# Gate projections token-major, in seven half-size products per branch, in a hybrid decoder block on one core

## The chip, the core and the metric

The kernel runs on one core of one Trainium2 chip. The metric is device microseconds of one execution. TensorE (PE) multiplies matrices, VectorE (DVE) and ScalarE (ACT) work on tiles, GpSimd (POOL) does the same and issues DMAs that add into a tile, SyncE (SP) issues the plain DMA loads. Times are in us unless marked ns.

## The reference

One layer over 512 tokens of 1024 channels. All weights and activations are float32.

```python
h = rms_norm(x, g_mix)
p = h @ w_in                       # 1024 -> 9*512 + 3*1024
q, fp, iv, go, bg, cg, xc, u, v, gates = split(p)
o_a, o_b, o_c = hgrn2(q, fp, iv, go), short_conv(bg, cg, xc), spatial_gate(u, v)
y = einsum('snw,nwd->snd', [o_a, o_b, o_c], w_branch)   # 3 branches, each 512 -> 1024
gate = sigmoid(gates).reshape(S, 3, 1024)
merged = sum(gate * y, axis=branch)
x = x + merged @ w_o
x = x + square(relu(rms_norm(x, g_ffn) @ w_ff1)) @ w_ff2
return rms_norm(x, g_final)
```

The change concerns `gates` (512 x 1024 by 1024 x 3072), `y` (three times 512 x 512 by 512 x 1024) and `merged`.

## The kernel before

**A float32 product in three.** Each operand is split into a high part, rounded to fp32r by a copy on ACT, and a low part, the rest, by a subtraction on DVE. `mm3` issues three matmuls: high by high, high by low, low by high. One matmul has a stationary block of 128x128 and moves 512 columns into a PSUM bank of 128x512.

**Units.** The kernel is a list `units`, worked off in order, each with a matmul part and a read-out for later. A usual unit is one 512 KB weight block: 8 blocks of 128x128, 24 matmuls. In order: units 0 to 3 and 4 to 7 (two projections of the recurrence), 8 to 11 (values), 12 to 15 (u), 16 to 19 (output gate), 20 to 31 (the convolution's three projections), and then, for each of the 8 blocks d of 128 output channels, five units: gate projections of branches 1, 2, 0 (24 matmuls each), `w_bc` (branches 1 and 2, 24) and `w_a` (branch 0, 12). These are units 32 to 71, channel-major: a tile is 128 channels by 512 tokens. `ev_gate` multiplies by the norm's factor `rb` and takes the sigmoid; `ev_bc` and `ev_a` multiply the branch results by the gates and add; `ev_a` leaves the merged tile split in high and low. The output projection (8 units) and the feed-forward part follow, the latter already in half-size products whose weight sums are added by DMA.

**Order of the queues.** It is written by hand (`manual_schedule`), so each engine does what the loop issues, in that order. For unit i the loop issues: the high split (ACT) of the weight block that a unit needs next, the read-out of unit i-1, the low split (DVE), other work hung on `pre`, one weight load (SP), the matmuls of unit i, and work hung on `post`. A weight block goes through a ring of three raw tiles and a ring of three pairs `wh`/`wl`; PSUM has eight banks (`acc`). Tiles named h, x, z and tmp are slots in fixed places that later stages use again, so a new owner waits until the last reader of the old one is done.

Of the kernel before, what the change touches and what calls it, by code (L numbers as in the profile page):

```python
# [7 lines left out]
F32 = mybir.dt.float32  # L8
# [3 lines left out]
ALU = mybir.AluOpType  # L12
# [21 lines left out]


@with_exitstack
def trunk_kernel(ctx: ExitStack, tc, xT, x_t, w_f, w_t, w_bc, w_a, w_o, w_1, w_2, vecs, rows, gfin, w_sg, cst, lmask, out):
# [22 lines left out]
    def zpair(i, dt):  # L60
        return rp.tile([P, 2 * S], dt, tag=f"z{i}", name=nm("z"))
# [59 lines left out]
    def tmp(w=S, dt=F32):  # L121
        return wp.tile([P, S + 64], dt, tag="tmp", name=nm("tmp"), bufs=6)[:, :w]
# [408 lines left out]
    def branch(w, o0, n):  # L531
        a = acc()
        for k in range(4):
            mm3(a, w[0][:, o0 + k * P:o0 + (k + 1) * P], w[1][:, o0 + k * P:o0 + (k + 1) * P],
                zt[n][k][0], zt[n][k][1], k == 0, k == 3)
        return a
# [6 lines left out]
    def ev_a(d, a):  # L543
        tt(dve, part[0], a, part[0], ALU.mult)
        tt(dve, part[0], part[0], part[1], ALU.add)
        mt = hslot(d, F32R)
        act.activation(mt[:, :S], part[0], AF.Copy)
        yield
        tt(dve, mt[:, S:], part[0], f(mt[:, :S]), ALU.subtract)
        mg.append((mt[:, :S], mt[:, S:]))  # L550


    for h in range(NH):
# [13 lines left out]
    for d in range(KD):  # L567
        for n in (1, 2, 0):
            proj(28 + n * KD + d, lambda a, d=d, n=n: ev_gate(d, n, a))
        unit(w_bc[d], lambda w: (branch(w, 0, 1), branch(w, S, 2)), lambda a, d=d: ev_bc(d, a))  # L570
        unit(w_a[d], lambda w: branch(w, 0, 0), lambda a, d=d: ev_a(d, a), S)

    at(pre, 3, sg_rows)
    at(pre, 4, sg_rows2)
# [39 lines left out]
    at(pre, 21, go_sig)  # L614


    x2, x2h, x2l = [], [], []
# [226 lines left out]
    at(pre, o0, reload_x)  # L844
    at(post, o0 + 4, turn, range(4))
    at(pre, o0 + 5, turned, range(4))
    f0 = len(units)
# [16 lines left out]
    at(pre, f0 + 4, ffn_rows)  # L864
    at(pre, f0 + 5, ev_1, 0)
    at(pre, f0 + 5, ev_1, 1)

    W11, W12, W21, W22 = (0, 0), (0, 1), (1, 0), (1, 1)

    def early(u):  # L870

# [91 lines left out]
    raws, ws = {}, {}  # L963
    order = [x for s in sorted(when) for x in when[s]]
    issued = [0]

    def issue():
        if issued[0] < len(order):
# [4 lines left out]
            issued[0] += 1  # L973

    def split_hi(i):
        n = loads[i][1]
# [198 lines left out]
```

## Time and profile before

| | us |
|---|---|
| runs | 829.84, 829.08, 829.73 |
| median of the runs | 829.73 |
| profiled execution, its own time | 829.28 |
| its span in the profile | 827.5 |
| PE busy | 816.4 (99%) |
| DVE busy | 544.0 (66%) |
| ACT busy | 346.0 (42%) |
| POOL busy | 156.7 (19%) |
| mean granted clock, of full speed | 0.997 |
| moved by DMA | 102.45 MB |

The span is that of one profiled execution on the chip; its own time is longer by what lies around the span. Matmuls overlap, so that PE counts as busy from the first to the last of a row without a gap. The order of reading is: which engine is busy, what the chain of work that ended last consists of, what that engine waited for, and then how full the others are in the stretch that is changed, here about 244 to 461 us after the start. Rows of all these views stand further down.

### The profile page before, as it was taken

Reading aid. Unit: us, or ns where it says so; the run is one execution under the profiler, and the core shown is the slowest. Engines: PE = TensorE matmul, PEld = TensorE weight load, DVE = VectorE, ACT = ScalarE, POOL = GpSimd, SP = SyncE. Lnnn points to the kernel's source line nnn. Section 1 sums busy time; section 2 is a strip of 40 time slices with the busy share of each in tenths; the row PEclk is TensorE's granted clock in tenths of the full one; section 3 lists DMA queues with packets and bytes.
Section 4 is the critical chain, followed back from the end, with each engine's and each line's share of the span. In section 5 each row is a group of like instructions: output and inputs, shape, how many; then the busy total and the mean of one; then the engine's idle time right before and its main releaser. Section 6 shows DMA issues by size and latency. Waiting matters only on the chain.

```text
span 827.5 us, 9867 instructions
## 1 busy us (share of the span) xinstructions
PE 816.4 (99%) x3798; PEld 680.7 (82%) x3798; DVE 544.0 (66%) x706; ACT 346.0 (42%) x519; POOL 156.7 (19%) x187
## 2 busy tenths in 40 slices
PE   9999999999999999999999999999999999999995
PEld 7888888888988888888888888888888888888884
DVE  7456999878664445544444445777777777777763
ACT  7467555364333223223232335343434343434332
POOL 4312644663220000000000010202020202020000
PEclk9999999999999999999999999999999999999998
DMA  8422222212122232222325345748384838383502
GB/s 309 127 80 75 76 102 77 77 52 95 60 63 103 91 113 90 90 93 98 115 89 204 103 160 145 216 115 231 99 222 113 248 85 251 83 250 87 162 0 102
DMA packets 30431, 102.45 MB, mean 124 GB/s; under 512 B 3504, under 2 KB 3888, under 8 KB 30384
## 3 DMA queue, kind: packets, MB, share of 16 engines
q1 hardware_dynamic: 20736, 67.45, 23.4%
q0 software_dynamic: 9360, 34.08, 16.7%
q8 instruction: 30, 0.49, 0.2%
q10 hardware_dynamic: 288, 0.29, 0.1%
q14 instruction: 17, 0.14, 0.1%
HBM read 99.71 MB, written 2.10 MB: 123 GB/s over the span
## 4 chain that ended last, share of the span: by engine, by line
PE 93%; DVE 3%; issue 2%; DMA 1%; ACT 0%; SPq 0%; POOLq 0%; POOL 0%; DVEq 0%
PE acc L98 29%; PE acc L99 29%; PE acc L100 29%; PE acc L330 2%; PE acc L1065 1%; DVE h L79 1%; DVE wl L79 1%; DVE h L307 1%; DMA raw<-w_t 1%; PE acc L485 0%; PE acc L386 0%; PE acc L648 0%; PE acc L388 0%; PE acc L369 0%; PE acc L328 0%
## 5 line engine op out<-in xcount | busy, mean ns | idle before, releaser
L98 PE MATMUL acc<-x,wh 128*128 128x512 f32 x672 | 263.9, 393 | 0.3 <-DVE h L339 0.3
L100 PE MATMUL acc<-x,wl 128*128 128x512 f32 x672 | 261.7, 389 | 0.0
L99 PE MATMUL acc<-x,wh 128*128 128x512 f32 x672 | 261.7, 389 | 0.0
L979 ACT ACTIVATE wh<-raw 128x1024 fp32r<-128x1024 f32 (+1 forms) x114 | 116.7, 1025 | 237.4 <-PE acc L99 134.6
L79 DVE TENSOR_TENSOR wl<-raw,wh 128x1024 fp32r<-128x1024 f32 (+1 forms) x120 | 153.6, 1282 | 44.0 <-ACT wh L979 43.9
L98 PEld LDWEIGHTS acc<-x,wh 128*128 128x128 f32 x672 | 126.2, 188 | 26.4 <-DVE h L339 0.5
L100 PEld LDWEIGHTS acc<-x,wl 128*128 128x128 f32 x672 | 126.2, 188 | 26.3
L99 PEld LDWEIGHTS acc<-x,wh 128*128 128x128 f32 x672 | 126.2, 188 | 25.6 <-issue 0.2
L79 DVE TENSOR_TENSOR h<-h,acc 128x512 f32<-128x512 f32 x118 | 75.7, 682 | 11.1 <-PE acc L100 11.0
L79 DVE TENSOR_TENSOR z<-z,z 128x1024 fp32r<-128x1024 f32 x51 | 61.6, 1220 | 32.1 <-ACT z L773 32.1
L79 DVE TENSOR_TENSOR h<-h,h 128x256 f32<-128x256 f32 (+4 forms) x89 | 67.9, 767 | 7.6 <-ACT h L752 3.6
L699 ACT ACTIVATE h<-tmp 128x512 f32<-128x512 f32 x32 | 20.3, 633 | 125.8 <-DVE tmp L698 125.8
L773 ACT ACTIVATE z<-z 128x1024 fp32r<-128x1024 f32 x51 | 53.1, 1052 | 44.8 <-PE acc L100 28.1
L100 PE MATMUL acc<-z,h 128*128 128x512 f32 x184 | 71.6, 389 | 0.0
L98 PE MATMUL acc<-z,h 128*128 128x512 f32 x184 | 71.6, 389 | 0.0
L99 PE MATMUL acc<-z,h 128*128 128x512 f32 x184 | 71.6, 389 | 0.0
L79 DVE TENSOR_TENSOR tmp<-acc,rb 128x512 f32<-128x512 f32 x28 | 19.4, 691 | 78.2 <-PE acc L100 78.2
L769 POOL DMA_DIRECT2D z<-w x28 | 24.5, 875 | 233.1 <-DVE z L79 194.5
L79 POOL TENSOR_TENSOR tmp<-tmp,tmp 128x512 f32<-128x512 f32 x15 | 19.9, 1324 | 198.8 <-DVE tmp L79 185.9
L698 DVE SCALAR_TENSOR_TENSOR tmp<-acc,rb 128x512 f32<-128x512 f32 x32 | 22.0, 688 | 30.8 <-PE acc L100 30.8
L98 PEld LDWEIGHTS acc<-z,h 128*128 128x128 f32 x184 | 34.5, 188 | 7.2
L100 PEld LDWEIGHTS acc<-z,h 128*128 128x128 f32 x184 | 34.5, 188 | 7.2
(190 smaller groups left out, 1066.3 us busy)
## 6 DMA issues: line engine op xcount, KB each, us to landing
z<-w POOLq DMA_DIRECT2D x65, 512.0 KB, 6.2
raw<-w_f SPq DMA_DIRECT2D x52, 512.0 KB, 3.2
raw<-w SPq DMA_DIRECT2D x34, 512.0 KB, 5.5
raw<-w_bc SPq DMA_DIRECT2D x8, 512.0 KB, 3.2
raw<-w_o SPq DMA_DIRECT2D x8, 512.0 KB, 3.3
raw<-w_t SPq DMA_DIRECT2D x4, 512.0 KB, 3.2
raw<-w_a SPq DMA_DIRECT2D x8, 256.0 KB, 2.6
h<-x_t SPq DMA_DIRECT2D x4, 512.0 KB, 6.8
```

The lines of the kernel that those rows point to most:

```text
L79: return e.tensor_tensor(out=o, in0=a, in1=b, op=op)
L98: pe.matmul(o, lh, rh, start=start, stop=False, skip_group_check=more)
L99: pe.matmul(o, lh, rl, start=False, stop=False, skip_group_check=more)
L100: pe.matmul(o, ll, rh, start=False, stop=stop, skip_group_check=more)
L307: dve.reciprocal(e[:, 256:], e[:, :256])
L330: pe.matmul(ps[:, cs(b)], kl[:, cs(b)], qk[:, cs(b)], start=True, stop=True)
L698: dve.scalar_tensor_tensor(out=t, in0=part["f", i], scalar=0.0, in1=part["r2b"], op0=ALU.max, op1=ALU.mult)
L699: act.activation(hf["a" if r < 2 else "b"][:, cs(r % 2, S)], t, AF.Square)
L769: pool.dma_start(wr[n, g], w_2[g, src[0], src[1]], accum_op=ALU.add)
L773: act.activation(hi, wr[src, g], AF.Copy)
L979: act.activation(hi[:, :n], raws[i][:, :n], AF.Copy)
L1065: pe.matmul(a4[t], lh, rh, start=j == 0 and rnd == 0, stop=j == KD - 1 and rnd == 2)
```

## The change

The gates and the branch products become token-major: a tile is 128 tokens by channels, x is the stationary operand and the weight moves. For each branch the gate projection is a 2 x 2 block product, 512 tokens by 1024 in halves, 1024 x 1024 weights in halves, done in seven products of half size (Strassen, in Winograd's form) with sums of the blocks of x and of the weights. With W11 to W22 for a branch's weight quarters, c is W12 to which W11, then W22, then W21 are added, and t3 is W12 plus W22. Each quarter is two raw blocks of 512 KB (g = 0, 1).

- **Order of the units.** Units 32 to 35 are the branch products of branch 1, 36 to 39 those of branch 2, both kept in SBUF. Units 40 to 46 are the seven gate products of branch 1, 47 to 53 of branch 2, 54 to 60 of branch 0, in the order p1, p5, p2, p6, p3, p7, p4 (weights W11, t1, W21, t2, W22, t3, t4, where t1, t2 and t4 are c after one, two and three additions, and p2 and p3 use raw quarters). Units 61 to 65 are branch 0's product, the last block of 24 matmuls cut into two units of 12. The output projection starts at unit 66.
- **x.** `x_load` fetches x again (8 loads), `x_norm` multiplies by weight and norm factor, `x_form` makes seven blocks or sums for each of two halves and splits them, hung on units 30 to 38.
- **Weights.** `g_load` loads raw quarters through the raw ring, `g_chain` starts c or t3 by a plain load, `g_add` adds a quarter by a DMA on POOL's queue, `g_split` splits one unit ahead of its product: three of four pairs in the rings `wh`/`wl`, the fourth in slots h0/h1. p1, p6, p7 and p4 add up in one pair of PSUM banks (B) and are read out in between, p5 and p3 in another (C), p2 has its own (A).
- **Read-out.** `g_ev` copies p1 and p5 to SBUF (`gt`), adds the next products to them and takes the sigmoid. `merge` multiplies a branch's kept product by its gates, `merge_add` adds two branches, `y_ev` of branch 0 multiplies and adds the last. `m_turn` turns the merged tiles by 32 transposes of 128x128 on PE, `m_turned` splits them.
- **Loads of later weights** stop at `phase1` and go on from unit 55 (`issue_more`).

In the diff "..." marks what is left out.

```diff
-    def ev_gate(d, n, a):
-        g = tmp()
-        part[n] = g
-        tt(dve, g, a, rb, ALU.mult)
-        act.activation(g, g, AF.Sigmoid)
...
-    def ev_bc(d, a):
-        for i, n in enumerate((1, 2)):
-            tt(dve, part[n], a[i], part[n], ALU.mult)
-        tt(pool, part[1], part[1], part[2], ALU.add)
...
+    def x_norm(g):
+        for b in range(4):
+            xv = xr_[b // 2][:, cs(b % 2, S)]
+            dve.scalar_tensor_tensor(out=xv, in0=xv, scalar=vcol(V_GMIX + 4 * g + b), in1=rb, op0=ALU.mult, op1=ALU.mult)
...
+    def x_form(g, *names):
...
+                i0, i1, op = {"1": (q(0, 1), q(1, 1), ALU.subtract), "2": (xr_.get("1"), q(0, 0), ALU.subtract),
+                              "4": (xr_.get("2"), q(1, 0), ALU.add), "3": (q(0, 0), q(0, 1), ALU.subtract)}[n]
+                tt(dve, src[n], i0, i1, op)
+        for n in names:
+            t = hslot(XT[g, n], F32R)
+            xf[g, n] = (two(t[:, :S]), two(t[:, S:]))
+            act.activation(xf[g, n][0], src[n], AF.Copy)
+        for n in names:
+            tt(dve, xf[g, n][1], src[n], f(xf[g, n][0]), ALU.subtract)
...
+    def g_chain(n, kind, base):
+        for g in range(2):
+            gw[n, g, kind] = xpair(base + g, F32)
+            nc.sync.dma_start(gw[n, g, kind], w_g[n, g, 0, 1])
+
+    def g_add(n, kind, fi, c):
+        for g in range(2):
+            pool.dma_start(gw[n, g, kind], w_g[n, g, fi, c], accum_op=ALU.add)
+
+    def g_split(n, name, src):
+        for g in range(2):
+            i = gn[0]
+            gn[0] += 1
+            if i % 4 < 3:
+                hi = wp.tile([P, 2 * S], F32R, tag="wh", name=nm("wh"))
+                lo = wp.tile([P, 2 * S], F32R, tag="wl", name=nm("wl"))
+            else:
+                hi, lo = hslot(0, F32R), hslot(1, F32R)
+            r = gw[(n, g) + src]
+            act.activation(hi, r, AF.Copy)
+            tt(dve, lo, r, f(hi), ALU.subtract)
...
+    def g_product(n, a, b, key, start):
...
+        for j in range(2):
+            for g in range(2):
+                for p in range(2):
...
+                    mm3(part[key][j], ah, al, bh, bl, start and g == 0 and p == 0, g == 1 and p == 1, not start)
+
+    G_ORDER = (("p1", "11", "11", "B", True), ("p5", "1", "t1", "C", True), ("p2", "12", "21", "A", True),
+               ("p6", "2", "t2", "B", False), ("p3", "4", "22", "C", False), ("p7", "3", "t3", "B", False),
+               ("p4", "22", "t4", "B", False))
...
+    def g_ev(p):
...
+            if p in ("p1", "p5"):
+                act.activation(v, a, AF.Copy)
+            elif p == "p6":
+                act.activation(v, a, AF.Copy, scale=-1.0)
+            elif p == "p4":
+                act.activation(v, a, AF.Sigmoid)
+            else:
+                tt(dve, v, v, a, ALU.subtract if p == "p7" else ALU.add)
+                act.activation(v, v, AF.Sigmoid)
...
+    def merge(v):
+        for t in range(4):
+            tt(dve, v[t], v[t], gt[t], ALU.mult)
...
+    def m_turn(ks):
+        for k in ks:
+            part["m", k] = acc()
+            for t in range(4):
+                pe.transpose(part["m", k][:, cs(t)], mt[t][:, cs(k)], ident)
...
+    def g_sched(n):
+        u = gu[n]
+        at(pre, u - 1, g_split, n, "11", W11)
+        at(pre, u, g_split, n, "t1", ("c",))
+        at(pre, u, g_add, n, "c", *W22)
+        at(pre, u + 1, g_split, n, "21", W21)
+        at(pre, u + 2, g_split, n, "t2", ("c",))
+        at(pre, u + 2, g_add, n, "c", *W21)
+        at(pre, u + 3, g_split, n, "22", W22)
+        at(pre, u + 4, g_split, n, "t3", ("t3",))
+        at(pre, u + 5, g_split, n, "t4", ("c",))
...
+    def g_early(n, s_c, s_t3, c, t3):
+        at(pre, s_c, g_chain, n, "c", c)
+        at(pre, s_c + 1, g_add, n, "c", *W11)
+        at(pre, s_t3, g_chain, n, "t3", t3)
+        at(pre, s_t3, g_add, n, "t3", *W22)
...
+    g_early(1, y2, y2 + 2, 4, 6)
...
+            at(pre, u2, merge, mt)
...
+            at(pre, u0, merge, yt)
+            at(pre, u0 + 1, merge_add)
...
+            L(u + 1, nxt, (0, W11))
+            L(u + 3, nxt, (1, W11), (0, W21))
+            g_early(nxt, u + 4, u + 6, c, t3)
```

The instructions below are in the order in which an engine takes them; names carry buffer numbers, `L` is a line of the kernel file. POOL before, from the last unit ahead of the gates: the tail of the spatial gate and the convolution, and then one addition of two branches for each d.

```order
L79 TENSOR_TENSOR rr_1979<-ra_1984,mhalf 128x4
L506 MEMSET tmp_2080 128x2
L79 TENSOR_TENSOR tmp_2083<-tmp_2083,rb 128x512
L79 TENSOR_TENSOR tmp_2162<-tmp_2162,tmp_2196 128x512
L79 TENSOR_TENSOR tmp_2323<-tmp_2323,tmp_2357 128x512
```

POOL after, for the gates of the second branch (unit 47 on): `x_2660` and `x_2662` are its c for g = 0 and 1, `x_2730` and `x_2732` its t3.

```order
L583 DMA x_2660<-w_g 128x1024
L583 DMA x_2662<-w_g 128x1024
L583 DMA x_2730<-w_g 128x1024
L583 DMA x_2732<-w_g 128x1024
L583 DMA x_2660<-w_g 128x1024
L583 DMA x_2662<-w_g 128x1024
```

The eight additions on tiles are gone, and each branch has eight DMAs that add: W11 into c, W22 into t3, W22 into c (these six are shown), and W21 into c behind them. The second addition into c stands behind those into t3 and is the one that t2 is split from.

DVE before, around one block d of the gates: read-outs of 512 columns, and one weight subtraction for a unit.

```order
L79 TENSOR_TENSOR wl_2711<-raw_2649,wh_2710 128x1024
L79 TENSOR_TENSOR tmp_2645<-acc_2719,tmp_2645 128x512
L79 TENSOR_TENSOR tmp_2679<-acc_2732,tmp_2679 128x512
L79 TENSOR_TENSOR wl_2746<-raw_2683,wh_2745 128x1024
L79 TENSOR_TENSOR tmp_2713<-acc_2754,tmp_2713 128x512
L79 TENSOR_TENSOR tmp_2713<-tmp_2713,tmp_2645 128x512
L79 TENSOR_TENSOR wl_2768<-raw_2717,wh_2767 128x1024
L79 TENSOR_TENSOR h_2772<-tmp_2713,h_2772 128x512
```

DVE after, at units 47 to 49, where the second branch begins: t1 (from `x_2660`, `x_2662`), the four products of the first branch's merge, W21, and t2 from the same two tiles.

```order
L85 TENSOR_TENSOR wl_2775<-x_2660,wh_2774 128x1024
L85 TENSOR_TENSOR wl_2779<-x_2662,wh_2778 128x1024
L85 TENSOR_TENSOR x_2213<-x_2213,z_2528 128x1024
L85 TENSOR_TENSOR x_2215<-x_2215,z_2529 128x1024
L85 TENSOR_TENSOR x_2217<-x_2217,z_2530 128x1024
L85 TENSOR_TENSOR x_2219<-x_2219,z_2531 128x1024
L85 TENSOR_TENSOR wl_2821<-raw_2624,wh_2820 128x1024
L85 TENSOR_TENSOR h_2825<-raw_2744,h_2824 128x1024
L85 TENSOR_TENSOR wl_2861<-x_2660,wh_2860 128x1024
L85 TENSOR_TENSOR wl_2865<-x_2662,wh_2864 128x1024
L85 TENSOR_TENSOR z_2814<-z_2814,acc_2870 128x512
```

A unit now has two weight subtractions, the merge's four products stand in one place ahead of W21's, and t2's ahead of the read-out of p2 (the last row).

## Rows read from the trace of the kernel before

**Rows 1.** The page's busy line, and its slices of PE, PE's clock and DMA:

```profile
PE 816.4 (99%) x3798; PEld 680.7 (82%) x3798; DVE 544.0 (66%) x706; ACT 346.0 (42%) x519; POOL 156.7 (19%) x187
...
PE   9999999999999999999999999999999999999995
...
PEclk9999999999999999999999999999999999999998
DMA  8422222212122232222325345748384838383502
```

**Rows 2.** The page's chain of work that ended last, by engine:

```profile
PE 93%; DVE 3%; issue 2%; DMA 1%; ACT 0%; SPq 0%; POOLq 0%; POOL 0%; DVEq 0%
```

**Rows 3.** What PE waited for: us in total, times, longest:

```profile
PE acc L996 <- DVE ones L989: 1.1, 1, 1.1
PE acc L1065 <- DVE wl L79: 0.6, 2, 0.4
PE acc L98 <- DVE h L339: 0.3, 1, 0.3
```

**Rows 4.** Timeline of PE, one gate unit: start, us, engine, line, operation:

```profile
243.94 0.39 PE L98 MATMUL acc<-x,wh 128*128 128x512 f32 x1
...
249.38 0.39 PE L98 MATMUL acc<-x,wh 128*128 128x512 f32 x1
```

**Rows 5.** The chain in order of time, the residual's turn: start, us, what:

```profile
468.51 1.75 PE acc L648 x16
```

**Rows 6.** Timelines of DVE and ACT; in brackets the idle time before:

```profile
247.29 0.68 DVE L79 TENSOR_TENSOR tmp<-acc,tmp 128x512 f32<-128x512 f32 x1
247.89 1.21 DVE L79 TENSOR_TENSOR wl<-raw,wh 128x1024 fp32r<-128x1024 f32 x1
249.02 0.69 DVE L79 TENSOR_TENSOR z<-tmp,z 128x512 fp32r<-128x512 f32 x1
...
261.92 1.06 ACT L979 ACTIVATE wh<-raw 128x1024 fp32r<-128x1024 f32 x1 [4.18 <-PE acc L100]
262.89 0.61 ACT L529 ACTIVATE tmp<-tmp 128x512 f32<-128x512 f32 x1
...
559.18 0.63 ACT L699 ACTIVATE h<-tmp 128x512 f32<-128x512 f32 x1 [4.00 <-DVE tmp L698]
559.72 1.05 ACT L752 ACTIVATE h<-h 128x1024 fp32r<-128x1024 f32 x1
```

**Rows 7.** Windows in the gate stage and the feed-forward stage:

```profile
core 0: us, PE busy (x) PEld busy (x) DVE busy (x) ACT busy (x) POOL busy (x), PEclk, DMA share, GB/s
...
283.00:322.00 39.00, 39.00 (x174) 32.31 (x173) 19.82 (x22) 11.54 (x14) 2.58 (x2) 1.00 0.29 95
591.00:595.50 4.50, 4.50 (x22) 3.72 (x21) 4.43 (x7) 4.50 (x6) 0.00 (x0) 1.00 0.36 117
591.00:634.50 43.50, 43.50 (x194) 36.02 (x193) 33.18 (x42) 19.52 (x24) 6.21 (x9) 1.00 0.59 160
```

**Rows 8.** Page's DMA issues; the adding line L769; ACT's timeline:

```profile
z<-w POOLq DMA_DIRECT2D x65, 512.0 KB, 6.2
raw<-w_f SPq DMA_DIRECT2D x52, 512.0 KB, 3.2
...
  DMA z<-w: 38.4, 11
...
  ACT z L773: 10.4, 7
...
DMA to landing us min/median/max: 5.2/5.9/10.6
...
563.86 1.06 ACT L773 ACTIVATE z<-z 128x1024 fp32r<-128x1024 f32 x1 [2.14 <-DMA z<-w]
```

More of the change, by code (lines that the diff above doesn't have):

```diff
@@ L543, in ev_a, with two @@
[L543 to L550, printed above, removed]
+    xr_ = {}
+    xf = {}
+    XT = dict(zip([(g, n) for g in range(2) for n in ("11", "12", "1", "2", "4", "3", "22")], range(2, 16)))
+    def two(ap):
+        return ap.rearrange("p (b c) -> p b c", b=2)
@@ new lines, in x_load, with q @@
+    def x_load(g):
+        for i in range(2):
+            xr_[i] = hslot(i, F32)
+            for b in range(2):
+                nc.sync.dma_start(xr_[i][:, cs(b, S)], xT[4 * g + 2 * i + b])
+    def x_norm(g):
[3 more added lines that the diff above has]
+    def x_form(g, *names):
+        def q(i, half):
+            return two(xr_[i])[:, :, half * 256:(half + 1) * 256]
+        src = {}
+        for n in names:
+            if n in ("11", "12", "22"):
+                src[n] = q(int(n[1]) - 1, int(n[0]) - 1)
+            else:
+                src[n] = xr_[n] = two(tmp())
+                i0, i1, op = {"1": (q(0, 1), q(1, 1), ALU.subtract), "2": (xr_.get("1"), q(0, 0), ALU.subtract),
[5 more added lines that the diff above has]
+            act.activation(xf[g, n][0], src[n], AF.Copy)
+        for n in names:
+            tt(dve, xf[g, n][1], src[n], f(xf[g, n][0]), ALU.subtract)
@@ new lines, in y_mm, with mm, y_ev @@
+    def y_mm(n, j, ks):
+        def mm(w):
+            if j == 0:
+                part["y"] = [acc() for _ in range(4)]
+            for k2 in ks:
+                k = 2 * j + k2
+                for t in range(4):
+                    mm3(part["y"][t], zt[n][k][0][:, cs(t)], zt[n][k][1][:, cs(t)], w[0][:, cs(k2, S)], w[1][:, cs(k2, S)],
+                        k == 0, k == 3)
+        return mm
+    def y_ev(n, c):
+        for t in range(4):
+            if n == 1 and c == 0:
+                mt[t] = xpair(t, F32)
+            if n == 2 and c == 0:
+                yt[t] = zpair(4 + t, F32)
+            v, m = (mt, yt, gt)[n - 1][t][:, cs(c, S)], mt[t][:, cs(c, S)]
+            if n:
+                act.activation(v, part["y"][t], AF.Copy)
+            else:
+                tt(dve, v, v, part["y"][t], ALU.mult)
+                tt(dve, m, m, v, ALU.add)
@@ new lines, in merge, with merge_add, m_turned @@
+    def merge(v):
+        for t in range(4):
+            tt(dve, v[t], v[t], gt[t], ALU.mult)
+    def merge_add():
+        for t in range(4):
+            tt(dve, mt[t], mt[t], yt[t], ALU.add)
+    def m_turn(ks):
+        for k in ks:
+            part["m", k] = acc()
+            for t in range(4):
+                pe.transpose(part["m", k][:, cs(t)], mt[t][:, cs(k)], ident)
+    def m_turned(ks):
+        for k in ks:
+            h = hslot(k, F32R)
+            act.activation(h[:, :S], part["m", k], AF.Copy)
+            tt(dve, h[:, S:], part["m", k], f(h[:, :S]), ALU.subtract)
+            mg.append((h[:, :S], h[:, S:]))
@@ L566, in trunk_kernel, with g_units @@
         proj(12 + c, lambda a, c=c: ev_bg(c, a))
[L567 to L571, printed above, removed]
+    y1 = len(units)
+    for c in range(2):
+        for j in range(2):
+            unit(w_b[1, c, j], y_mm(1, j, range(2)), (lambda a, c=c: y_ev(1, c)) if j else None)
+    y2 = len(units)
+    for c in range(2):
+        for j in range(2):
+            unit(w_b[2, c, j], y_mm(2, j, range(2)), (lambda a, c=c: y_ev(2, c)) if j else None)
+    phase1 = len(loads)
+    gu = {}
+    def g_units(n):
+        gu[n] = len(units)
+        for o in G_ORDER:
+            units.append((None, lambda w, o=o: g_product(n, *o[1:]), lambda a, o=o: g_ev(o[0])))
+    g_units(1)
+    g_units(2)
+    g_units(0)
+    y0 = len(units)
+    for c in range(2):
+        for j in range(2):
+            if c and j:
+                load(len(units) - 2, w_b[0, c, j])
+                units.append((len(loads) - 1, y_mm(0, j, range(1)), None))
+                units.append((len(loads) - 1, y_mm(0, j, range(1, 2)), lambda a, c=c: y_ev(0, c)))
+            else:
+                load(len(units) - 1 if c == 0 else len(units) - 2, w_b[0, c, j])
+                units.append((len(loads) - 1, y_mm(0, j, range(2)), (lambda a, c=c: y_ev(0, c)) if j else None))
     at(pre, 3, sg_rows)
@@ L614, in trunk_kernel, with L @@
     at(pre, 21, go_sig)
+    at(pre, y1 - 2, x_load, 0)
+    at(pre, y1 - 1, x_norm, 0)
+    at(pre, y1, x_form, 0, "11", "1")
+    at(pre, y1 + 1, x_form, 0, "2", "12")
+    at(pre, y1 + 2, x_form, 0, "4", "3", "22")
+    at(pre, y1 + 2, x_load, 1)
+    at(pre, y1 + 3, x_norm, 1)
+    at(pre, y1 + 4, x_form, 1, "11", "1")
+    at(pre, y1 + 5, x_form, 1, "2", "12")
+    at(pre, y1 + 6, x_form, 1, "4", "3", "22")
+    W11, W12, W21, W22 = (0, 0), (0, 1), (1, 0), (1, 1)
+    def L(slot, n, *what):
+        for g, w in what:
+            at(pre, slot, g_load, n, g, *w)
+    def g_sched(n):
[9 more added lines that the diff above has]
+        at(pre, u + 5, g_split, n, "t4", ("c",))
+        at(pre, u - 1, g_load, n, 1, *W21)
+        at(pre, u - 1, g_load, n, 0, *W22)
+        at(pre, u + 1, g_load, n, 1, *W22)
+    def g_early(n, s_c, s_t3, c, t3):
[3 more added lines that the diff above has]
+        at(pre, s_t3, g_add, n, "t3", *W22)
+    u1, u2, u0 = gu[1], gu[2], gu[0]
+    L(y2 + 1, 1, (0, W11), (1, W11), (0, W21))
+    g_early(1, y2, y2 + 2, 4, 6)
+    for n, u, nxt, c, t3 in ((1, u1, 2, 6, 4), (2, u2, 0, 4, 6), (0, u0, None, 0, 0)):
+        g_sched(n)
+        if n == 2:
+            at(pre, u2, merge, mt)
+        elif n == 0:
+            at(pre, u0, merge, yt)
+            at(pre, u0 + 1, merge_add)
+        if nxt is not None:
+            L(u + 1, nxt, (0, W11))
+            L(u + 3, nxt, (1, W11), (0, W21))
+            g_early(nxt, u + 4, u + 6, c, t3)
     x2, x2h, x2l = [], [], []
@@ L866, in trunk_kernel @@
     at(pre, f0 + 5, ev_1, 1)
-    W11, W12, W21, W22 = (0, 0), (0, 1), (1, 0), (1, 1)
     def early(u):
@@ L965, in trunk_kernel @@
     issued = [0]
+    limit = [phase1]
     def issue():
-        if issued[0] < len(order):
+        if issued[0] < limit[0]:
             src, n = loads[order[issued[0]]]
@@ L973, in issue, with issue_more @@
             issued[0] += 1
+    def issue_more(n):
+        limit[0] = len(order)
+        for _ in range(n):
+            issue()
+    at(pre, u0 + 1, issue_more, 1)
+    at(pre, u0 + 3, issue_more, 2)
     def split_hi(i):
```

52 lines of the change are left out of this document (36 added, 16 removed).

## The prediction

> **What bounds the kernel now.** I read the page's busy line first: TensorE is busy 816.4 of 827.5 us and its clock digit stays at 9, the upper of its two levels (2.4 GHz), until the last slice [rows 1]. The chain of work that ended last gives 93% to PE [rows 2], and the list of what PE waited for holds three entries, 2.0 us in all, none of them in the gate stage [rows 3]. In the gate stage PE is busy 39.00 of 39.00 us, DVE 19.82, ACT 11.54, and the DMA engines 0.29 of their time [rows 7]. So the kernel is as long as its matmuls, the other queues have room, and two questions decide: how many matmuls go, and whether the work that feeds the new ones arrives in time.
>
> **The matmuls.** One 128x512 matmul starts every 5.44/24 = 0.2267 us: the two rows lie 24 matmuls, one unit, apart [rows 4]. Units 32 to 71 of before issue 576 gate matmuls and 288 branch matmuls. Of the gates, seven half-size products replace eight: 3 branches x 7 products x 24 = 504, so 72 go; the branch products keep their 288 in another order. 72 x 0.2267 = 16.3 us, all on the path. Added on TensorE are 32 transposes of 128x128; sixteen of the same kind in the residual's turn take 1.75 us [rows 5], so 32 take 3.5 us. **Net on TensorE: -12.8 us.** The profiled execution took 829.28 us (span 827.5 and 1.8 around it), 0.45 below the median of the runs, so the floor of the changed kernel is 816.5 by that execution and 816.9 by the median.
>
> **The splits beside it.** A product unit lasts 5.44 us and needs two 1024-wide splits for the next unit. On ACT a 1024-wide copy occupies 0.97 us, a 512-wide one 0.54; on DVE a 1024-wide subtraction occupies 1.13 us, a 512-wide one about 0.6 [rows 6]. Per unit that is at most 2 x 0.97 + 2 x 0.54 = 3.0 us of ACT and 2 x 1.13 + 2 x 0.6 = 3.5 us of DVE, under 5.44. But the buffers hold two units, so a split for unit i+1 waits until unit i-1 has let its pair go: the chain read-out, copy, subtraction must fit into one unit. With a read-out that passes DVE and ACT it is 0.2 + 0.6 + 0.6 + 0.54 + 2 x 0.97 + 1.22 = 5.1 us for the second half, needed 1.6 us into the unit: 1.9 us to spare. I cost it at nothing.
>
> Where a branch ends, DVE also has the four merge products of 1024 (4 x 1.13 = 4.5 us): the splits of the following unit then end at 10.0 and 11.2 us after the branch's first unit began, needed at 11.1 and 12.5, so about 1 us is left. At the third branch four merge additions follow, and the next split ends at 16.9 where 16.5 is wanted: 0.4 us late, 0 to 0.4 in the sum. One wait is new: product 4 adds onto the two banks that product 7 has just filled. The first bank is full half a unit earlier, but its read-out on DVE stands behind the two t4 subtractions and ends about 5.5 us into a unit of 5.44: 0.1 us, three times, 0.3 us; bounds 0 and, if the whole read-out were exposed, 3 x 0.7 = 2.1.
>
> The forms of x (8 norms, 8 differences, 14 subtractions on DVE, 14 copies on ACT, 8 loads of 256 KB) lie beside units 30 to 39. In unit 31 DVE has 10.4 us of work and enters unit 32 some 4 us late; its first result that TensorE wants is the last half of the convolution branch, halfway through unit 33. About 1.5 us are to spare, so nothing; without that cover it costs what it is late, once. SP is moved too: the x loads stand in its queue ahead of the branch weights, which are issued over a unit before their split. The 8 additions that POOL did on tiles go; they were off the path. The turned merge tiles (ACT copy, DVE subtraction) are made under the last branch unit and under the first output unit.
>
> **The adds, which I do price.** Per branch SP issues 10 loads of 512 KB (six raw blocks, two first blocks for the chain c, two for t3) and POOL issues 8 loads that add into a tile (W11, W22, W21 into c, W22 into t3, for two halves g). The trace has both kinds. In the gate stage 0.29 x 39 = 11.3 us of engine time moved 95 GB/s x 39 us = 3.7 MB, seven loads: 1.6 us each; one load by itself gives 0.36 x 4.5 = 1.6 [rows 7]. Eight units of the feed-forward stage hold nine loads and four adds: 0.59 x 43.5 = 25.7, less 9 x 1.6, leaves 2.8 us for an add [rows 7]. So a branch wants 10 x 1.6 + 8 x 2.8 = 38.4 us of the DMA engines, and lasts 7 x 5.44 = 38.1. They would go from 0.29 to full, and what comes last in their queue comes late.
>
> That is t2, the fourth product. Take the first unit of the second branch as time 0. The subtractions of the previous t3 end near -13.3 and -12.2 and free the tile of the new c; its loads land 3.2 us later [rows 8], at -10.1 and -9.0. From there the engines have in a row: W11 into c (two adds), the first blocks of t3 (two loads), two raw loads, W22 into t3 (two adds), W22 into c (two adds, issued at +3.1 and +4.2, behind t3's in POOL's queue). That is 6 x 2.8 + 4 x 1.6 = 23.2 us, and an add alone takes 5.2 us from issue to landing [rows 8], 2.4 more than its engine time: the last lands at -10.1 + 23.2 + 2.4 = +15.5 if nothing comes between, and two more raw loads are issued from +9.9 and may come between: +18.7. TensorE wants the second half's t2 at 16.3 + 6 x 0.2267 + 0.2 = 17.9, copy and subtraction take 2.3, so it must have landed by +15.6. Late by 0 to 3.1 us. The lower bound for the whole effect is nothing: if the transfers did not queue, t3 would land at once and W22 into c at +8.3 and +11.1. The nearest rows are those of a full queue: in the feed-forward stage, where only one add stands between the splits, ACT already waits for an add, 10.4 us over seven times, 2.14 in the row shown, and POOL waits 38.4 us over eleven for one before the next [rows 8]. So I take the middle of 0 to 3.1, 1.6 us, at each of two switches (the first branch's chains start under the branch products, where the engines are idle): 3.2 us.
>
> The Trainium skill (DMA: Bandwidth & Descriptors, Anatomy of one DMA) prices a transfer at about 2.0 us and its bytes at 436 GB/s, 3.2 us for 512 KB, and names no surcharge for adding. The load rows agree, 3.2 us; the add rows do not, 5.2 at least [rows 8]. By that price the branch would need some 22 us of engine time and t2 would be in time; the sum would be 816.9.
>
> **Sum**, on the median: 829.73 - 16.3 + 3.5 + 3.2 = **820.1 us**; the 0.3 and 0.4 of the read-outs fall where TensorE then waits anyway or are inside the rounding. Bounds of the unknowns: 0 and 6.2 us for t2, 0 and 2.1 for product 4, 0 and 0.4 for the merge.
>
> **The rivals.** *All hidden* (0.25): the adds keep up, as the spare of 0.1 us at the early end would have it; -12.8 us, 816.5 to 817.5. For it speaks that shares of packet time count waiting too, so 2.8 us may be too much. *Adds late as priced* (0.48): 0.5 to 6.5 us, 817.5 to 823.5. *More than priced* (0.18): the loads wait behind adds as well and stretch the chain at the front, or product 4 exposes its read-out; 6.5 to 11 us, 823.5 to 828.1.
>
> *Slower* (0.05): the adds become the bound of the stage. One mechanism, at the same place: each pair of adds lands late by what the worst row shows. A pair should take 5.2 + 2.8 = 8.0 us; the longest single add took 10.6 [rows 8], 2.6 more. Three pairs in the chain give 7.8, with the 1.6 above 9.4 per switch, 18.8 for two: 829.73 - 12.8 + 18.8 = 835.7. It decides from (6.4 - 1.6)/3 = 1.6 us per pair; against it speaks that the median add takes 5.9.
>
> The Trainium skill (DMA: Bandwidth & Descriptors, Latency and other measured facts) says that two of the sixteen DMA engines are usually slower, with descriptors built by GpSimd as the likely cause. That would be this rival, 835.7 us where it held every time; no row here tells the engines apart, and the 10.6 us is the only one that hints at it.
>
> *It does not do what it says*: the products are back to back in code, but the fourth of a branch may start late and the seventh waits for a read-out; this is inside the cases above and can at most undo the gain.
>
> **How the numbers follow.** Likeliest is the priced case, 820.1. No change within 0.2% (828.1 to 831.4, about what a measurement of this kernel can tell from no change) would need 11 to 14 us of waits: 0.04. The range runs from the hidden case to two thirds of the heavy one, 816.4 to 825.5, which leaves out 0.18. Faster 0.91, same 0.04, slower 0.05.
>
> **What would show it.** Right: 40 matmul instructions fewer (72 go, 32 transposes come), DMA share near 0.9 or more from the first to the third gate branch, two PE waits of 1 to 3 us on ACT or DVE at the fourth product of branches 2 and 0, whose ACT copy itself waits for an add. If these waits are missing, the price of the adds was too high; if TensorE waits at every product, the one-unit split chain was cut too close; if a wait stands at units 32 to 36, the forms of x were not hidden. The forecast would be wrong if the granted clock fell to its lower level after a wait: the gate stage shows 1.00 throughout [rows 7].

## The result and the profile after

The changed kernel takes 818.84 us (median of four runs, 817.87 to 820.44) beside 829.52 of the kernel before: 10.7 us less, ratio 0.9881, 95% interval 0.987 to 0.9893. The ratio is estimated over the single runs and is not the quotient of the medians (0.9871); it stands for 9.9 us less, its interval for 8.9 to 10.8. The forecast was 820.1 in a range of 816.4 to 825.5. A second set of runs gave 818.77 beside 828.26, 9.5 us less, ratio 0.9884 (0.987 to 0.9897).

The profiled execution took 817.87 us, span 816.1. These lines of its page, and of its list of PE's waits, answer to [rows 1 to 3]:

```profile
PE 804.6 (99%) x3758; PEld 669.9 (82%) x3758; DVE 572.4 (70%) x740; ACT 386.0 (47%) x581; POOL 169.5 (21%) x203
...
DMA  8421232212232998989344255848383838393502
...
PE 87%; DVE 4%; ACT 3%; DMA 2%; issue 2%; POOL 0%; POOLq 0%; ACTq 0%; DVEq 0%
...
PE acc L105 <- DVE wl L85: 1.5, 2, 1.1
PE acc L1211 <- DVE ones L1204: 1.1, 1, 1.1
PE acc L104 <- DVE h L345: 0.3, 1, 0.3
```

PE has 40 instructions fewer (72 matmuls gone, 32 transposes come) and 11.8 us less to do. The DMA line has six slices of 8 and 9 in a row, 265 to 388 us, from the first additions on, where before it had 2 and 3. The wait list names 1.5 us at two matmuls. That is not all: a row of a matmul lasts 0.39 us and the next starts 0.2267 later, so a gap shorter than that overlap shows only in the starts. So I take the distance from one matmul's start to the next, less 0.2267 us, and add what the following one is still late by. The timeline of PE after, at four places (start, length, operation):

```profile
319.88 0.39 PE L106 MATMUL acc<-h,h 128*128 128x512 f32 x1
320.31 0.47 PE L104 MATMUL acc<-wh,h 128*128 128x512 f32 x1
320.62 0.39 PE L105 MATMUL acc<-wl,h 128*128 128x512 f32 x1
...
336.74 0.39 PE L104 MATMUL acc<-wh,h 128*128 128x512 f32 x1
337.12 0.50 PE L105 MATMUL acc<-wl,h 128*128 128x512 f32 x1
...
343.82 0.39 PE L104 MATMUL acc<-wh,h 128*128 128x512 f32 x1
344.61 0.50 PE L105 MATMUL acc<-wl,h 128*128 128x512 f32 x1 [0.40 <-DVE wl L85]
...
381.63 0.39 PE L104 MATMUL acc<-wh,h 128*128 128x512 f32 x1
383.11 0.50 PE L105 MATMUL acc<-wl,h 128*128 128x512 f32 x1 [1.09 <-DVE wl L85]
```

320.31 is the start of p4 (branch 1), 0.43 after the matmul ahead of it: 0.28 us lost with the next one, and as much at p4 of the other two branches. 337.12 is p2 of branch 2 (0.25 us), 344.61 p6 of branch 2 (0.67), 383.11 p6 of branch 0 (1.35). Together 3.1 us; everything else from unit 32 to the residual's turn runs without a gap over 0.04 us but for the transposes. Those are, in the chain in order of time:

```profile
424.30 1.75 PE acc L672 x16
...
434.23 1.75 PE acc L672 x16
...
457.76 1.75 PE acc L855 x16
```

The first two are the 32 transposes, 2 x 1.75 = 3.5 us, as [rows 5] had it; the third is the residual's turn. So the stage gives -16.3 + 3.5 + 3.1 = -9.7 us. The two profiled executions differ by 11.4, but that of before was 1.36 us late already where the conv units end (under a2_after_again below), and the two differ by 0.7 behind the last matmul; the residual's turn comes 10.75 us earlier (457.76 instead of 468.51), and 10.75 - 1.36 = 9.4, 0.3 from the sum.

### The profile page after: what moved, and what is told of

Its sections match the earlier page's. It is cut to its first block, busy times and chain, and to the rows that moved or that the text cites. A ratio compares the mean times of both kernels' runs of the same rounds, so it can differ in the third digit from the quotient of the medians.

```text
span 816.1 us, 9971 instructions
## 1 busy us (share of the span) xinstructions
PE 804.6 (99%) x3758; PEld 669.9 (82%) x3758; DVE 572.4 (70%) x740; ACT 386.0 (47%) x581; POOL 169.5 (21%) x203
## 4 chain that ended last, share of the span: by engine, by line
PE 87%; DVE 4%; ACT 3%; DMA 2%; issue 2%; POOL 0%; POOLq 0%; ACTq 0%; DVEq 0%
PE acc L105 26%; PE acc L104 26%; PE acc L106 26%; PE acc L1280 3%; DMA x<-w_g 2%; PE acc L336 2%; DVE wl L85 1%; DVE h L85 1%; DVE h L313 1%; ACT h L263 1%; DVE h L276 0%; ACT wh L1194 0%; PE acc L1211 0%; ACT h L267 0%; PE acc L491 0%
## 5 line engine op out<-in xcount | busy, mean ns | idle before, releaser
L104 PE MATMUL acc<-x,wh 128*128 128x512 f32 x480 | 189.1, 394 | 0.3 <-DVE h L345 0.3
L106 PE MATMUL acc<-x,wl 128*128 128x512 f32 x480 | 186.9, 389 | 0.0
L105 PE MATMUL acc<-x,wh 128*128 128x512 f32 x480 | 186.9, 389 | 0.0
L1194 ACT ACTIVATE wh<-raw 128x1024 fp32r<-128x1024 f32 x86 | 90.3, 1053 | 139.7 <-PE acc L105 44.3
L104 PEld LDWEIGHTS acc<-x,wh 128*128 128x128 f32 x480 | 90.2, 188 | 18.9 <-DVE h L345 0.5
L106 PEld LDWEIGHTS acc<-x,wl 128*128 128x128 f32 x480 | 90.1, 188 | 18.8
L105 PEld LDWEIGHTS acc<-x,wh 128*128 128x128 f32 x480 | 90.2, 188 | 18.4 <-issue 0.2
L85 DVE TENSOR_TENSOR z<-z,z 128x1024 fp32r<-128x1024 f32 (+1 forms) x55 | 66.3, 1220 | 32.1 <-ACT z L977 32.1
L105 PE MATMUL acc<-wl,h 128*128 128x512 f32 x208 | 81.3, 391 | 1.5 <-DVE wl L85 1.5
L104 PE MATMUL acc<-wh,h 128*128 128x512 f32 x208 | 81.4, 391 | 0.1
L106 PE MATMUL acc<-wh,h 128*128 128x512 f32 x208 | 81.0, 389 | 0.0
L105 PEld LDWEIGHTS acc<-wl,h 128*128 128x128 f32 x208 | 39.1, 188 | 10.8 <-DVE wl L85 2.9
L104 PEld LDWEIGHTS acc<-wh,h 128*128 128x128 f32 x208 | 39.0, 188 | 9.3 <-issue 0.9
```

Of the source, the lines that this page charges most:

```text
L1194: act.activation(hi[:, :n], raws[i][:, :n], AF.Copy)
```

## Who makes PE wait

The gate products of branch 2 begin at 325.83 (unit 47), those of branch 0 at 365.25 (unit 54). ACT's timeline after, the copies that start a split:

```profile
329.06 1.06 ACT L595 ACTIVATE wh<-x 128x1024 fp32r<-128x1024 f32 x1 [1.46 <-DMA x<-w_g]
...
342.24 1.06 ACT L595 ACTIVATE wh<-x 128x1024 fp32r<-128x1024 f32 x1 [1.91 <-DMA x<-w_g]
...
368.25 1.06 ACT L595 ACTIVATE h<-x 128x1024 fp32r<-128x1024 f32 x1 [1.22 <-DMA x<-w_g]
...
378.14 1.06 ACT L595 ACTIVATE wh<-x 128x1024 fp32r<-128x1024 f32 x1 [1.13 <-DMA x<-w_g]
...
380.96 1.06 ACT L595 ACTIVATE h<-x 128x1024 fp32r<-128x1024 f32 x1 [1.75 <-DMA x<-w_g]
```

342.24 is t2 of branch 2, second half: its add is there 16.4 us after the branch began, the prediction wanted it by 15.6, and PE is late by 0.67. This is the wait that was forecast. 329.06 and 368.25 are t1, second half, and that was not: the second add of W11 into c is there only about 3 us after the branch has begun. What it does is seen on DVE, branch 0:

```profile
369.34 1.22 DVE L85 TENSOR_TENSOR h<-x,h 128x1024 fp32r<-128x1024 f32 x1 [1.05 <-ACT h L595]
370.48 4.62 DVE L85 TENSOR_TENSOR z<-z,z 128x1024 f32<-128x1024 f32 x4
375.02 2.35 DVE L85 TENSOR_TENSOR wl<-raw,wh 128x1024 fp32r<-128x1024 f32 x2
377.30 4.62 DVE L85 TENSOR_TENSOR x<-x,z 128x1024 f32<-128x1024 f32 x4
381.84 1.21 DVE L85 TENSOR_TENSOR wl<-x,wh 128x1024 fp32r<-128x1024 f32 x1
```

From t1's late subtraction DVE works without a gap: merge products, W21's split, merge additions, and only then t2's first subtraction, at 381.84, whose copy on ACT had ended at 379.2. It ends 17.8 us after the branch's start and is wanted at 16.5. So in branch 0 the releaser is DVE's row, though the second half's add was just in time: its copy starts at 380.96, 15.7 after the start.

## The experiments

Waits are read from the starts as above, in us, in the one profiled execution of each kernel; b2 and b0 are branches 2 and 0. "Less" is the median against the median of before in the same set: 828.26 for a2 and e1 to e3, 829.34 for f1 to f4, 828.14 for f5 and f6. Kernels of different sets are compared by the ratio, estimated as above. e1, e2 and e3 leave out a part of the output.

| kernel | p4, three | p2 b2 / b0 | p6 b2 | p6 b0 | sum | median | less | ratio, interval |
|---|---|---|---|---|---|---|---|---|
| after | 0.83 | 0.25 / 0 | 0.67 | 1.35 | 3.1 | 818.84 | 10.7 | 0.9881 (0.987-0.9893) |
| a2_after_again | 0.82 | 0.46 / 0.21 | 0.66 | 1.35 | 3.5 | 818.77 | 9.5 | 0.9884 (0.987-0.9897) |
| e1_no_adds | 0.82 | 0 / 0 | 0 | 0.24 | 1.1 | 817.09 | 11.2 | 0.9863 (0.985-0.9877) |
| e2_plain_pool | 0.82 | 0 / 0 | 0 | 0.23 | 1.1 | 816.48 | 11.8 | 0.9846 (0.9832-0.986) |
| e3_no_merge | 0.82 | 0 / 0 | 2.29 | 1.79 | 4.9 | 820.04 | 8.2 | 0.9898 (0.988-0.9917) |
| f1_t3_later | 0.83 | 0.37 / 0 | 0 | 1.25 | 2.5 | 817.73 | 11.6 | 0.9862 (0.9847-0.9877) |
| f2_mid_read | 0 | 0.72 / 1.08 | 0.68 | 1.34 | 3.8 | 819.94 | 9.4 | 0.9895 (0.9876-0.9913) |
| f3_add_spread | 2.1 | 0.27 / 0.94 | 1.18 | 0 | 4.5 | 818.47 | 10.9 | 0.9878 (0.9865-0.9892) |
| f4_all | 0.42 | 0.46 / 0.26 | 0 | 0 | 1.1 | 816.25 | 13.1 | 0.9849 (0.9836-0.9863) |
| f6_base_alone | 0.81 | 0 / 0 | 0 | 0.24 | 1.1 | 816.63 | 11.5 | 0.9854 (0.984-0.9867) |
| f5_base_later | 0.41 | 0 / 0 | 0 | 0 | 0.4 | 815.79 | 12.4 | 0.9842 (0.9829-0.9856) |

**The changed kernel again.**

> The changed kernel once more, to see what of the profiled execution repeats. In that execution TensorE's waits in the gate stage were 0.26 us (p2 of branch 2), 0.68 and 1.36 us (p6, whose weight is t2, of branches 2 and 0) and three times 0.28 us (p4): 3.1 us. It also began unit 32 1.36 us earlier than the kernel before did, by waits at 15 and 18 us that only the kernel before had. Theory A (the adds that land late set the waits at p2 and p6): the three p4 waits repeat to 0.05 us, those at p2 and p6 move by 0.5 us and more with the landing times. Theory B (DVE's row of merge products and additions sets them): all repeat to 0.1 us. Theory C (the early start is chance of an execution): the wait at 15 to 19 us is there in some executions of either kernel; the rival, that the change starts earlier, has it never. Median 818.8, ratio 0.987 to 0.989.

The six waits repeat, a seventh of 0.21 us at p2 of branch 0 comes to them; the late p6 of branch 0 repeats to 0.01 us, p2's moves by 0.2. So neither sign came: the waits at p2 and p6 moved by 0.2 us at most, less than theory A wanted, and p2's by more than theory B allowed. The early beginning is chance. The same matmul of unit 31, ahead of anything that differs, starts at these times in before, after, a2_after_again, e1_no_adds and f5_base_later:

```profile
239.77 0.48 PE L98 MATMUL acc<-x,wh 128*128 128x512 f32 x1
...
238.41 0.48 PE L104 MATMUL acc<-x,wh 128*128 128x512 f32 x1
...
238.76 0.48 PE L104 MATMUL acc<-x,wh 128*128 128x512 f32 x1
...
240.07 0.48 PE L104 MATMUL acc<-x,wh 128*128 128x512 f32 x1
...
240.72 0.48 PE L104 MATMUL acc<-x,wh 128*128 128x512 f32 x1
```

Over 2 us of a single execution's time are decided before the change begins, in kernels that are the same up to there, so the waits in the stage are compared below, not single times. The waits at p2 and p6 differ between executions too, as f3 shows below.

**Without the adds, and with the adds as plain loads.**

```diff
     def g_add(n, kind, fi, c):          # e1_no_adds
-        for g in range(2):
-            pool.dma_start(gw[n, g, kind], w_g[n, g, fi, c], accum_op=ALU.add)
+        return
...
-            pool.dma_start(gw[n, g, kind], w_g[n, g, fi, c], accum_op=ALU.add)
+            pool.dma_start(gw[n, g, kind], w_g[n, g, fi, c])       # e2_plain_pool
```

> Leaves out the 24 additions by DMA: c and t3 stay plain W12, so the gates are computed from wrong weight sums; all products, splits, read-outs and merges stay. Theory A: the waits at p2 and p6 go, at most 0.4 us stays at p6 of branch 0 behind the merge additions, the three p4 waits of 0.28 us stay; 1.9 to 2.3 us less than the changed kernel, 816.6 to 817.0, DMA share of the stage under 0.6. Theory B: the DVE row alone keeps 0.9 us or more at p6 of branch 0 and 0.2 at p2; under 1.2 us less.

> The same 24 transfers on POOL's queue with the same waits, but overwriting instead of adding, so the weight sums are left out. The prediction put an addition at 2.8 us of the DMA engines and a load at 1.6. If adding is what costs: landing falls from 7.7 us (median) to 4 to 6, the DMA share of the gate branches from 0.9 to about 0.75, waits at p2 and p6 fall to 0.5 us or less, 816.6 to 817.2. If a transfer on that queue costs the same whether it adds or not: landing about 7.7, share 0.9, waits 1.5 to 2.5 us, within 0.5 us of the changed kernel.

Both lose the waits at p2 and at p6 of branch 2; 0.24 us stays at p6 of branch 0, behind the merge additions, as theory A had it. Beside their own before they gain 11.2 and 11.8 us where a2 gains 9.5, so 1.7 and 2.3 more; 1.9 to 2.3 was expected of e1. In e2 the transfers, their queue and their bytes are those of the changed kernel; what is gone is the adding, and with it some of POOL's issuing time (0.53 us for each instead of 0.86). Windows that hold all 24 transfers from issue to landing, of after, e1_no_adds and e2_plain_pool:

```profile
268.00:405.00 137.00, 135.39 (x591) 110.09 (x590) 85.07 (x86) 79.77 (x106) 20.96 (x24) 1.00 0.87 224
...
268.00:405.00 137.00, 136.88 (x600) 112.18 (x600) 86.79 (x89) 79.20 (x107) 0.00 (x0) 1.00 0.41 136
...
268.00:405.00 137.00, 136.88 (x601) 112.15 (x600) 85.74 (x88) 79.24 (x107) 12.90 (x24) 1.00 0.67 227
```

The last three columns are clock, DMA share and GB/s; POOL's count is the transfers issued there. An add takes (0.87 - 0.41) x 137 / 24 = 2.6 us of the sixteen engines, the same transfer without adding (0.67 - 0.41) x 137 / 24 = 1.5. The prediction had 2.8 and 1.6. From issue to landing, POOL's line of after and then of e2:

```profile
DMA to landing us min/median/max: 5.1/7.7/10.7
...
DMA to landing us min/median/max: 3.3/5.3/8.0
```

The Trainium skill (Collectives: The Full Stack, The bandwidth ceiling: the fold count and why AG ≠ RS ≠ AR) says of ReduceScatter, in rings of three or more ranks, that it runs at half the rate of AllGather because its add needs two source reads, and gives a measured ratio of 1.93. That is a collective and not a kernel's own transfer; the ratio here, 2.6 to 1.5 or about 1.8, is near it, but no run shows that the second read is the cause.

**Without the merge.**

```diff
     def merge(v):
-        for t in range(4):
-            tt(dve, v[t], v[t], gt[t], ALU.mult)
+        return
...
     def merge_add():
-        for t in range(4):
-            tt(dve, mt[t], mt[t], yt[t], ALU.add)
+        return
```

> Leaves out the eight merge products and the four merge additions of 1024 on DVE, so the output lacks the sums over branches. Theory A alone: p6 of branch 2 still waits 0.5 us or more for its add, p6 of branch 0 up to 0.3 us (its add landed just in time), p2 nothing; about 1.5 us less than the changed kernel. Theory B alone: no wait at p2 or p6; 2.3 us less. In both the three p4 waits of 0.28 us stay.

Both theories missed: with DVE busy for 13 us less (559.7 instead of 572.4), the waits at p6 grew from 2.0 to 4.1 us and the time is no shorter than that of the changed kernel. ACT's copy for t2 of branch 2 in e3, and SP's next two raw loads in e3 and in after:

```profile
343.98 1.06 ACT L595 ACTIVATE wh<-x 128x1024 fp32r<-128x1024 f32 x1 [2.81 <-DMA x<-w_g]
...
334.73 1.46 SPq L574 DMA_DIRECT2D raw<-w_g  x2
...
337.09 1.46 SPq L574 DMA_DIRECT2D raw<-w_g  x2
```

W21's split no longer stands behind the merge, lets its raw tiles go 2.4 us earlier by these rows, and SP issues two raw loads for much later products while the adds into c are still under way. The copy starts at 343.98 instead of 342.24, 17.8 us after the branch's start instead of 16.4. I read this as: the merge had held back transfers that the adds now share the engines with. That is argued and not shown: no run takes these early loads away again, and in branch 2 of e3 the first addition into t3 was also issued later, 328.90 instead of 324.81, closer to those into c.

**t3's adds behind c's.**

```diff
-        at(pre, s_t3, g_add, n, "t3", *W22)
+        at(pre, gu[n] + 1, g_add, n, "t3", *W22)
```

> Output complete. The two additions into t3 are issued after those of W22 into c (POOL's order changes, the count of transfers doesn't). Theory D (the adds of one branch queue: what stands ahead of W22 into c in POOL's queue and in the DMA engines sets the waits): the second add of W22 into c lands 3 to 5.7 us earlier (two adds at 2.8 us), at about +10 to +13 after the branch's first unit, before the 15.6 at which it is wanted; p6 waits nothing in branch 2 and 0.25 us in branch 0, p2 at most 0.3; 1.5 to 2.3 us less than the changed kernel. Rival E (the engines are simply full: whatever stands later is late in turn): the wait moves to t3 at p7 or t4 at p4, 0.5 us or more there, and the time stays within 0.7 us.

Half of theory D holds: p6 of branch 2 waits nothing, the wait has not moved to p7 or p4, so the engines are not simply full. The 0.25 us for branch 0 was wrong, 1.25 stays, with DVE as its releaser: the merge additions end at 382.9, t2's subtraction follows. The add alone was not the cause there.

**p7's read-out in between.**

```diff
...
+    def g_mid(n):
+        v, a = gt[2][:, cs(1, S)], part["B"][0]
+        tt(dve, v, v, a, ALU.subtract)
+        hi, lo = gw[n, 1, "t4", "r"]
+        tt(dve, lo, gw[n, 1, "c"], f(hi), ALU.subtract)
+        act.activation(v, v, AF.Sigmoid)
...
-        at(pre, u + 5, g_split, n, "t4", ("c",))
+        at(pre, u + 5, g_split_t4, n)
+        at(post, u + 5, g_mid, n)
```

> Output complete. The read-out of p7's first bank stands ahead of t4's second subtraction on DVE instead of behind both. If the place in DVE's queue makes the 0.28 us at p4, these three waits go and nothing else moves: 0.8 us less than the changed kernel. If the bank itself is the limit (p7's results not there earlier), the 0.28 us stays.

The three waits at p4 are gone, so the place in DVE's queue made them. But p2 of branches 2 and 0 went from 0.25 and 0 to 0.72 and 1.08, and the time is no shorter. The 0.28 us won ahead of a switch is lost there again if the W11 add and the merge come no sooner; the rest can be chance, for p2 of branch 0 was 0.94 in f3, whose edit lies behind it.

```profile
378.70 0.50 PE L105 MATMUL acc<-wl,h 128*128 128x512 f32 x1 [0.81 <-DVE wl L85]
```

That is p2 of branch 0 in f2.

**The merge additions spread.**

```diff
...
-            at(pre, u0 + 1, merge_add)
+            for t in range(4):
+                at(pre, u0 + 3 + t, merge_add, t)
```

> Output complete. The four merge additions of the third branch stand one by one at units 57 to 60 instead of together at unit 55, ahead of t2's subtractions. If they are what TensorE waited for at p6 of branch 0 (1.35 us), that wait falls to 0.3 us or less, 1.0 us less than the changed kernel. If, as where all merge work was left out, a freer DVE releases raw tiles earlier and loads come between the adds, the add lands later and the wait stays at 0.8 to 1.8 us.

The wait at p6 of branch 0 is gone, so the additions made it. The gain was not had: in the profiled execution, the slowest of its four, 0.94 us stands at p2 of branch 0 and 1.18 at p6 of branch 2. Neither comes from the edit, which moves only what stands behind these places in DVE's order; in this execution the second W11 add was late, by ACT's copy for t1 of branch 0. So a wait at p2 or p6 can change by 0.5 to 0.9 us from one execution to another. What the edit did add is at p4, which waits for p7's read-out; that has the last addition ahead of it on DVE:

```profile
370.99 1.06 ACT L595 ACTIVATE h<-x 128x1024 fp32r<-128x1024 f32 x1 [2.15 <-DMA x<-w_g]
...
402.20 0.47 PE L104 MATMUL acc<-wh,h 128*128 128x512 f32 x1 [1.31 <-DVE z L85]
```

**All three.**

> Output complete. All three edits at once. Theory D: no wait over 0.1 us is left in the gate stage, except up to 0.3 at p2; the stage costs 12.8 us less than before, 3.2 to 3.5 us less than the changed kernel, 815.3 to 815.8 beside 828.3 to 829.5 of before, ratio 0.984 to 0.985. Rival E: 1 us or more of waits stays at p7 or p4.

816.25 us, 13.1 less than before; 1.1 us of waits stay, 0.72 of them at p2. More than the 0.3 expected there: p2 is the place that the three edits do not touch.

**Where p2's wait starts.** In f4 as in after, the second W11 add lands 10 us after its issue, and t3's first two loads are issued beside it. POOL and SP after, branch 2:

```profile
318.32 0.87 POOL L583 DMA_DIRECT2D x<-w_g  x1 [0.38 <-issue]
...
318.46 1.46 SPq L579 DMA_DIRECT2D x<-w_g  x2
```

The next two kernels issue these loads a unit later (at 327.10 in f6): f6 with the edit of f1 alone, f5 with all three:

```diff
-        at(pre, s_t3, g_chain, n, "t3", t3)
+        at(pre, gu[n], g_chain, n, "t3", t3)
```

> Output complete. As f1_t3_later, and t3's two first loads are issued a unit later too, so that they no longer stand beside the additions of W11 into c. Theory F (the late start: the second addition of W11 lands 10 us after its issue because t3's loads are moved at the same time; t1's second split waits for it, then the merge products, W21's split and in branch 0 the merge additions are late in a row): ACT no longer waits for the add at t1, the second t1 subtraction ends by +4.5 instead of +5.6 us after the branch's first unit, p2 waits nothing, p6 of branch 0 at most 0.3 us instead of 1.25; 1.4 to 2.0 us less than f1_t3_later, near 816.0 to 816.6. Rival G (DVE's merge work alone makes p6 of branch 0 late): 0.9 us or more stays there.

> Output complete. f4_all with t3's first loads a unit later. Theory F: the waits at p2 (0.46 and 0.26 us in f4_all) go, no wait over 0.15 us is left in the gate stage but up to 0.4 at p4 of branch 0; 0.5 to 0.8 us less than f4_all, 815.4 to 815.8. Rival G: within 0.2 us of f4_all.

In f6 the waits at p2 and p6 go but for 0.24 us, the merge staying where it was. ACT no longer waits for t1, and in branch 0 the merge additions start 10.9 us after the branch does (365.89 in f6) instead of 12.05. ACT in branch 2 and in branch 0, then DVE in branch 0:

```profile
328.24 2.00 ACT L595 ACTIVATE wh<-x 128x1024 fp32r<-128x1024 f32 x2
...
367.55 1.05 ACT L595 ACTIVATE h<-x 128x1024 fp32r<-128x1024 f32 x1
...
376.78 4.62 DVE L85 TENSOR_TENSOR x<-x,z 128x1024 f32<-128x1024 f32 x4
381.32 1.22 DVE L85 TENSOR_TENSOR wl<-x,wh 128x1024 fp32r<-128x1024 f32 x1
```

t2's first subtraction ends 16.6 us after the start instead of 17.8: theory F. Rival G falls. One execution would not be enough for this, but the sign is the same in each: in after, a2 and f1 to f4 ACT waits 1.1 to 2.3 us for the second W11 add at all twelve switches, in f5 and f6 at none of four. By the times alone f6 and f1 could not be told apart (816.63 and 817.73, ratios 0.9854 and 0.9862 with overlapping intervals, and 11.5 and 11.6 us less than their own before, where 1.4 to 2.0 us between them were expected), nor f5 and f4; the waits tell them apart. f5 has the lowest median and ratio, 815.79 us beside 828.14, 12.4 less, ratio 0.9842 (0.9829 to 0.9856); its interval lies clear of that of the changed kernel. One wait of 0.41 us is left in the gate stage, at p4 of branch 0, which shows as 0.2 in the list of what PE waited for; the other three entries lie outside the stage:

```profile
PE acc L1224 <- DVE ones L1217: 1.1, 1, 1.1
PE acc L1293 <- DVE wh L1260: 0.5, 1, 0.5
PE acc L104 <- DVE h L345: 0.3, 1, 0.3
PE acc L104 <- DVE z L85: 0.2, 1, 0.2
```

## Why the prediction was right, and where it was not

**The matmuls, -16.3 us, and the transposes, +3.5**, stand. In f5, where 0.4 us of waits is left, 12.8 - 0.4 = 12.4 us should be missing. From the matmul of unit 31 shown above to the residual's turn the kernel before takes 468.51 - 239.77 = 228.7 us [rows 5], f5 takes 216.4, 12.3 less. Its row of the residual's turn:

```profile
457.15 1.75 PE acc L868 x16
```

**The adds' price.** 2.8 us was worked out from the feed-forward stage [rows 7]; e1 and e2 give 2.6, and 1.5 without adding. By these a branch wants 10 x 1.5 + 8 x 2.6 = 36 us of the engines in 38.1, so they are nearly full, not full. By the Trainium skill's price (DMA: Bandwidth & Descriptors, Anatomy of one DMA) the sum was 816.9, with t2 in time; e2, where the same transfers do not add and land in 3.3 us at the least, has t2 in time; the changed kernel, with 5.1 at the least, has not. The clock stayed at its upper level, 1.00 in every window shown.

**The waits, +3.2**, were 3.1 and 3.5 us in two executions. The size is right, the make-up only in part, and part of the agreement is luck. Of the two waits of 1 to 3 us that were to show the forecast right, one came in that size:

- p6 of branch 2 was put at 1.6 us, by an add that lands at 15.5 to 18.7 where 15.6 was wanted. The copy started at 16.4, 0.8 late, and PE lost 0.67. The mechanism is right, for with t3's adds behind (f1) this wait is gone; the middle of the range was too high.
- p6 of branch 0 was put at 1.6 for the same reason. It lost 1.35, but to the merge additions; the add was there at 15.7, about when it was wanted. The prediction had these additions 0.4 us late and dropped them as falling where TensorE waits anyway. It was the other way round, since their row began late: the step that failed is t1, which the prediction took to be in time. Its row of transfers had W11's adds first and t3's loads behind them; the engines moved both at once, and ACT waited 1.46 and 1.22 us for the second add. With t1 in time (e2, f6) 0.24 stays, inside the 0 to 0.4 that was named.
- p2 of branch 2, with 1 us to spare by the prediction, lost 0.25 to 0.46, from the same late t1.
- p4 was 0.1 us three times and was left out as hidden; it is 0.28 three times and adds up, 0.83 us. The read-out was rightly named; a wait of it is followed by a matmul that is 0.08 late, and nothing later absorbed it.

**What lay beside** did stay there: no gap at units 32 to 39, so the forms of x were hidden, none at the turned tiles.

**The slower rival**, 2.6 us more for each pair of adds, did not come. Landings of 10 us and more were seen for the second add of a pair, like the 10.6 of [rows 8], but the chain still ended at 16.4 and 15.7 us. The Trainium skill's two slow DMA engines (DMA: Bandwidth & Descriptors, Latency and other measured facts) stay open: no run here tells the engines apart.

**The range.** Its upper end, 825.5, is called two thirds of the heavy case; of 823.5 to 828.1 it takes in 2.0 of 4.6 us, under half.

**Left open.** Whether the 9.5 and 10.7 us of the two sets differ at all: the ratios, 0.9884 and 0.9881, do not. How much of the scatter is the beginning and how much the landings of single executions; the four runs of the changed kernel lie 2.6 us apart, and only one of each set has a profile. The medians of the table differ from 12.8 less the waits beside them by up to 1.4 us (f4), in f3, whose profile is of its slowest run, by 2.6.

## What to carry to other kernels

When a product is saved by sums that the DMA engines make, cost the sums in engine time (here an add took about 1.8 times a plain transfer) and follow the first of them, not the last: the late start of a chain moves every step that stands behind it in an in-order queue. Edits at later places of the chain took their own waits away but left the late start, and with it 0.4 to 1.8 us at p2 (f1 to f4); the edit where the chain begins left none there (f5, f6), and f6, which moves t3's loads and adds alone, has 1.1 us of waits in all, as much as f4 with its three edits. Before taking work away from an engine that is not the bottleneck, ask which buffers it will free and what will be loaded into them: e3 suggests that this work can keep transfers apart, though no run here isolates it. And where single executions differ by as much as the waits under study, ask of each changed wait whether the edit can reach it at all (f3).

## What was not expected of the hardware

An adding DMA of 512 KB took 2.6 us of the sixteen engines beside 1.5 for the same transfer without adding, 5.1 us at least from issue to landing beside 3.3. Less work on DVE made the kernel no faster: e3 has 13 us less of it and 4.1 us of waits at p6 instead of 2.0.
